# Latent attention in pairs of heads: weights normalised on GpSimd, values stationary in the two column halves of TensorE

## The chip, the cores and the metric

The kernel runs on one core of one Trainium2 chip. A core has TensorE (matrix products; PE in the profile, with PEld for the loading of its stationary operand), VectorE (DVE), ScalarE (ACT), GpSimd (POOL), SyncE (SP, which issues the loads here) and 16 DMA engines. Matrix products are written to PSUM, in banks of 128 partitions by 512 floats. Everything else lies in SBUF. The metric is the device time of one execution in microseconds (us), lower is better.

## The reference

Two decoder layers on 512 positions of width 1024, in float32. Each layer is a feed-forward network, a token mixer and a second feed-forward network, each between RMS norms. The mixer of the first layer is multi-head latent attention, and only that mixer is touched:

```python
def causal_block_attention(q, k, v, scale):      # 512 positions, 16 heads, q and k 96 wide, v 64 wide
    ...
    def one_block(args):                         # 128 queries at a time
        qi, n = args
        s = jnp.einsum('bhqd,bhkd->bhqk', qi, kt).astype(jnp.float32) * scale
        qpos = n * Q_BLOCK + jnp.arange(Q_BLOCK)
        s = jnp.where(kpos[None, :] <= qpos[:, None], s, -jnp.inf)
        p = jax.nn.softmax(s, axis=-1).astype(vt.dtype)
        return jnp.einsum('bhqk,bhkd->bhqd', p, vt)
    ...

def mla(h, w_in, q_norm, w_q_up, kv_norm, w_kv_up, w_o):
    ...
    o = causal_block_attention(q, k, v, (QK_NOPE + QK_ROPE) ** -0.5)
    return o.reshape(B, S, MLA_HEADS * V_HEAD) @ w_o
```

## The kernel before

Activations are kept transposed: a tile has 128 features in its partitions and the 512 positions in its columns. The big products (lines 121 to 123, `mm3`) split each float32 operand into a rounded part and a rest and add three products in the fast type fp32r. The latent attention's own products, its scores, transposes and weighted sums, are plain float32: the compiler makes two passes of each float32 product, and one of a transpose.

The stage begins with `values` (lines 606 to 618), which puts the values of all 16 heads in SBUF as tiles `v`, with 128 positions in the partitions and 64 columns for a head. `keys` (620 to 650) makes the queries and keys of four heads at a time, in five units: one of them, `rope`, has a multiplication on POOL (line 641) for which DVE waits (line 644), and the pairs with keys copy the rotary part on POOL (line 634). `rest` (717 to 736) walks through the heads. For each head it calls `attend` four times, for the query blocks i = 0 to 3. Block i has 128 queries and, since attention is causal, n = 128(i + 1) keys. Between these calls it lets `keys` for the next four heads go on by a unit (after every second call: `KQ`).

`attend` cuts the work on a block into steps that `Pipe(1)` puts one call apart:

- `score` (660 to 669): the product of queries and keys on PE into a bank `mm`, one DVE instruction that scales, masks and finds the row's maximum (666, with a short read of the accumulator), and the exponential on ACT, which also sums the row (669, again with a read of the accumulator). The result is in a tile `sq` (four buffers), with queries in the partitions.
- `turn` (671 to 681): i + 1 transposes on PE into a bank `aux` (676), and a copy to SBUF, on DVE for i < 3 (681) and on ACT for i = 3 (679).
- `weigh` (683 to 705): i + 1 products on PE with a turned 128x128 block of weights as the stationary operand and 64 columns of `v` as the moving one (687). The 128 queries stand in the partitions of the result. After i = 3, DVE takes the reciprocals of the four row sums (696) and multiplies the head's whole output by them (700) into half of a tile `acc`.
- `close` (707 to 713): after every second head, four transposes of `acc` on PE (712) and `put_o` (540 to 546), which splits the result in its rounded part (ACT, 543) and rest (DVE, 544) for the output product.

`rest` then goes on with the output product (`out_unit`), which needs the outputs of all heads. The order of instructions on each engine is set at build time by a scheduler of the framework, which moves instructions past one another as their data allow. Each engine then runs its own queue in that order.

In the second layer the dilated attention has products (line 872) that use 64 of TensorE's 128 rows, a head in each half, and a multiplication on POOL by a broadcast operand (line 985). The change does not touch them, but the prediction reads their prices.

Of the kernel before, what the change touches and what calls it, by code (L numbers as in the profile page):

```python
# [7 lines left out]
F32 = mybir.dt.float32  # L8
F32R = mybir.dt.float32r
AF = mybir.ActivationFunctionType  # L10
ALU = mybir.AluOpType
# [16 lines left out]
KQ = 2  # L28
# [520 lines left out]
class Mla(Mixer):  # L549
# [102 lines left out]
    def attend(self, h, q, k, pipe, at):  # L652
        t, nc = self.t, self.t.nc
        sc = 96.0**-0.5
        if at == 0:
            self.st = t.tmp.tile([P, 8], F32, tag="st", name="st", bufs=3), {}
        st, box = self.st
        nm, z = st[:, 0:4], st[:, 4:8]

        def score(i):  # L660
            n = (i + 1) * P
            c = slice(i, i + 1)
            s = t.bank()[:, :n]
            nc.tensor.matmul(s, q[0:96, i * P : n], k[0:96, :n], start=True, stop=True)  # L664
            p = box[i] = t.t("sq", SB)[:, :n]
            nc.vector.tensor_tensor_reduce(
                p, s, self.mask[:, SEQ - n :], -sc, 3e38, ALU.add, ALU.min, accum_out=nm[:, c]
            )
            nc.scalar.activation(p, p, AF.Exp, bias=nm[:, c], scale=-1.0, accum_out=z[:, c])

        def turn(i):
            n = (i + 1) * P
            x = t.bank("aux")[:, :n]
            for j in range(i + 1):
                r = slice(j * P, (j + 1) * P)
                nc.tensor.transpose(x[:, r], box[i][:, r], t.ident)  # L676
            box[i] = t.t("silu" if i % 2 else "gg")[:, :n]
            if i == 3:
                nc.scalar.activation(box[i], x, AF.Copy)
            else:  # L680
                nc.vector.tensor_copy(box[i], x)

        def weigh(i):
            if i == 0:
                box["o"] = t.bank("aux")
            for j in range(i + 1):
                nc.tensor.matmul(  # L687
                    box["o"][:, i * 64 : i * 64 + 64],
                    box[i][:, j * P : (j + 1) * P],
                    self.v[j, h // 8][:, (h % 8) * 64 : (h % 8) * 64 + 64],  # L690
                    start=j == 0,
                    stop=j == i,
                )
            if i < 3:
                return
            nc.vector.reciprocal(z, z)
            if h % 2 == 0:
                self.os = t.t("acc")
            dst = self.os.rearrange("p (i e c) -> p i e c", i=4, e=2)[:, :, h % 2, :]
            nc.vector.tensor_tensor(  # L700
                dst,
# [438 lines left out]
```

## Time and profile before

| | |
|---|---|
| median of 3 runs | 2410.98 us (2410.79 to 2415.25) |
| span of the profiled execution | 2412.5 us, 0.06% above the median |
| the attention's blocks, first score to last transposes of the output | about 474 to 602 us of the span |
| TensorE busy over the span | 2348.5 us (97%) |
| mean granted TensorE clock | 0.990 |

The page and the trace give no time beside the span, so the span is taken as the profiled execution's own time. Two cautions on reading them. A matmul's recorded duration contains its way through the array, which the next one overlaps: what one costs in a dense stream is the distance between the starts of neighbours. And rows of the time line are merged: `x8` is eight passes in a row that begin at the time given, and the next row's start tells when the stream has moved on.

### The profile page before, as it was taken

How to read it: one execution, taken by the hardware profiler on the slowest of the kernel's cores; microseconds unless marked ns; L12 is line 12 of the kernel's file. 1: busy time of each engine (PE TensorE's matmuls, PEld its weight loads, DVE VectorE, ACT ScalarE, POOL GpSimd, SP SyncE). 2: the span in 40 equal slices, each digit the busy share in tenths (PEclk: the TensorE clock that was granted, in tenths of full speed). 3: DMA queues.
4: the chain of work that ended last, by engine and by line, in shares of the span. 5: the costliest groups of instructions: out<-in, count | busy, mean ns of one | idle time of the engine just before them, and what ended most of it. 6: DMA issues, size and time to landing. Idle time of an engine off the chain costs nothing.

```text
span 2412.5 us, 32825 instructions
## 1 busy us (share of the span) xinstructions
PE 2348.5 (97%) x12430; PEld 1995.6 (83%) x12430; DVE 1235.7 (51%) x2863; ACT 867.2 (36%) x1743; POOL 226.8 (9%) x264
## 2 busy tenths in 40 slices
PE   6999999999999999999999999999999999999998
PEld 5888888778888888888888887888888888888887
DVE  8735536688464454485454364443334456423333
ACT  3422224455432222342222254443334445322221
POOL 0000004210320000230000130000000004100002
PEclk9999999899999999999999999999999998999999
DMA  7645431422245453245454222222222212322221
GB/s 298 220 153 168 158 98 64 151 81 89 70 158 174 151 173 125 68 149 175 148 179 144 89 75 87 70 78 87 87 64 77 88 52 71 105 96 89 104 87 36
DMA packets 104770, 279.46 MB, mean 116 GB/s; under 512 B 28561, under 2 KB 34980, under 8 KB 104612
## 3 DMA queue, kind: packets, MB, share of 16 engines
q1 hardware_dynamic: 104612, 277.36, 35.3%
q8 instruction: 98, 1.61, 0.3%
q14 instruction: 60, 0.49, 0.1%
HBM read 274.95 MB, written 2.37 MB: 115 GB/s over the span
## 4 chain that ended last, share of the span: by engine, by line
PE 89%; DVE 4%; POOL 3%; issue 1%; ACT 1%; DMA 1%; SPq 0%; POOLq 0%; ACTq 0%; DVEq 0%
PE mm L121 26%; PE mm L122 26%; PE mm L123 26%; PE mm L872 2%; PE aux L920 2%; PE mm L664 1%; PE aux L687 1%; PE aux L907 1%; POOL rs L216 1%; DVE x L363 1%; DVE s L360 1%; PE aux L219 1%; PE aux L676 1%; DMA s<-w_mod 1%; POOL sq L250 1%
## 5 line engine op out<-in xcount | busy, mean ns | idle before, releaser
L121 PE MATMUL mm<-s,whi 128*128 128x512 f32 (+1 forms) x3344 | 1214.2, 365 | 8.2 <-ACT whi L104 3.2
L122 PE MATMUL mm<-s,whi 128*128 128x512 f32 (+1 forms) x3344 | 1214.2, 364 | 2.4 <-POOL s L276 1.9
L123 PE MATMUL mm<-s,wlo 128*128 128x512 f32 (+1 forms) x3344 | 1210.1, 363 | 0.0
L104 ACT ACTIVATE whi<-raw 128x1024 fp32r<-128x1024 f32 (+1 forms) x374 | 387.9, 1038 | 1195.1 <-PE mm L122 903.9
L106 DVE TENSOR_TENSOR wlo<-raw,whi 128x512 fp32r<-128x512 f32 (+1 forms) x748 | 489.2, 689 | 538.8 <-ACT whi L104 534.0
L121 PEld LDWEIGHTS mm<-s,whi 128*128 128x128 f32 x3344 | 635.2, 190 | 107.6 <-ACT whi L104 4.0
L122 PEld LDWEIGHTS mm<-s,whi 128*128 128x128 f32 x3344 | 636.4, 190 | 98.7 <-POOL s L276 4.0
L123 PEld LDWEIGHTS mm<-s,wlo 128*128 128x128 f32 x3344 | 635.9, 190 | 94.3 <-DVE wlo L106 0.8
L129 DVE CUSTOM_DVE_ANT_0 raw<-raw,cs 128x1024 f32<-128x1024 f32 x128 | 157.5, 1232 | 147.4 <-DMA raw<-w_mod 146.9
L376 POOL TENSOR_TENSOR acc<-acc,sq 128x256 f32<-128x256 f32 (+1 forms) x60 | 57.5, 959 | 1394.1 <-ACT sq L230 1393.0
L450 DVE TENSOR_TENSOR gg<-silu,mm 128x512 f32<-128x512 f32 (+1 forms) x95 | 60.4, 636 | 174.2 <-PE mm L123 172.5
L476 DVE TENSOR_TENSOR s<-mm,s 128x512 f32<-128x512 f32 (+1 forms) x84 | 47.3, 563 | 144.3 <-PE mm L123 143.8
L887 ACT ACTIVATE sq<-sq,dst 128x128 f32<-128x128 f32 x192 | 79.7, 418 | 8.8 <-DVE dst L880 7.6
L273 ACT ACTIVATE s<-u,mS 128x256 fp32r<-128x256 f32 (+1 forms) x88 | 42.6, 518 | 57.2 <-DVE u L269 57.2
L451 ACT ACTIVATE s<-gg 128x512 fp32r<-128x512 f32 (+1 forms) x97 | 57.4, 592 | 15.3 <-DVE gg L450 13.5
L872 PE MATMUL mm<-s 64*128 64x128 f32 (+1 forms) x384 | 62.7, 321 | 0.0
L230 ACT ACTIVATE sq<-s 128x256 f32<-128x256 f32 (+1 forms) x82 | 35.9, 444 | 59.9 <-DVE s L476 56.9
L453 DVE TENSOR_TENSOR s<-gg,s 128x512 fp32r<-128x512 f32 x79 | 54.2, 686 | 0.3
L880 DVE CUSTOM_DVE_ANT_0 sq<-mm,s 128x128 f32<-128x128 f32 x192 | 51.7, 318 | 4.1 <-PE mm L872 4.1
L448 ACT ACTIVATE silu<-mm 128x512 f32<-128x512 f32 (+1 forms) x95 | 51.3, 540 | 6.4 <-PE mm L123 6.3
L872 PEld LDWEIGHTS mm<-s 64*128 64x128 f32 x384 | 44.1, 186 | 10.8 <-issue 3.4
L363 DVE TENSOR_TENSOR x<-x,s 128x256 f32<-128x256 f32 x90 | 50.0, 586 | 0.0
(149 smaller groups left out, 1542.3 us busy)
## 6 DMA issues: line engine op xcount, KB each, us to landing
raw<-w_gu SPq DMA_DIRECT2D x176, 512.0 KB, 3.3
raw<-w_mod SPq DMA_DIRECT2D x128, 512.0 KB, 3.3
raw<-dil_in SPq DMA_DIRECT2D x72, 512.0 KB, 3.2
raw<-w_down SPq DMA_DIRECT2D x64, 448.0 KB, 3.3
raw<-w_down SPq DMA_DIRECT2D x32, 512.0 KB, 3.6
s<-w_mod SPq DMA_DIRECT2D x32, 256.0 KB, 7.2
raw<-mla_o SPq DMA_DIRECT2D x8, 512.0 KB, 3.7
raw<-dil_o SPq DMA_DIRECT2D x8, 512.0 KB, 3.3
```

What stands on the lines that cost most here:

```text
L104: self.nc.scalar.activation(hi, raw, AF.Copy)
L106: self.nc.vector.tensor_tensor(lo[:, r], raw[:, r], f(hi[:, r]), ALU.subtract)
L121: mm(out, w[0], m[0], start=first, stop=False)
L122: mm(out, w[0], m[1], start=False, stop=False)
L123: mm(out, w[1], m[0], start=False, stop=last)
L129: nc.vector.tensor_tensor_reduce(raw, raw, self.cs, 1.0, 0.0, ALU.mult, ALU.add, accum_out=t[:, 0:1])
L363: eng.tensor_tensor(self.x[:, k, lo:hi], self.x[:, k, lo:hi], yk, ALU.add)
L376: nc.gpsimd.tensor_tensor(acc, acc, self.sq(yk, n), ALU.add)
L450: nc.vector.tensor_tensor(v, s, banks[1], ALU.mult)
L451: nc.scalar.activation(ghi, v, AF.Copy)
L872: nc.tensor.matmul(s[:, at : at + n], q[rows, i * P : (i + 1) * P], k[rows, k0 : k0 + n], start=True, stop=True)
L887: nc.scalar.activation(y[:, c], y[:, c], AF.Exp, bias=st[:, g, i, e : e + 1], scale=-1.0, accum_out=st[:, g, i, 2 + e : 3 + e],)
```

## The change

Heads are worked on in pairs, and `attend` is called for a pair c and a block i.

- `score` makes both heads' scores, maxima and exponentials. Then DVE takes the reciprocals of both row sums, and POOL multiplies each `sq` tile by its reciprocal, broadcast along the row. The weights are thus normalised before they are turned.
- `turn` turns both heads' weights, into tiles `silu` (first head) and `gg` (second).
- `weigh` has 64 columns of `v` as the stationary operand and the turned weights, 128 queries, as the moving one. The first head's result goes to partitions 0 to 63 of the bank and the second's to 64 to 127, so that each head uses one half of TensorE's columns. The result has features in its partitions and 128 queries in its columns, and after i = 3 `put_o` reads it as it is: the step `close`, its transposes, and the multiplication of line 700 are gone.
- `rest` calls `keys` on after each of the eight calls for a group of four heads (before: after every second of sixteen).

```diff
-    def attend(self, h, q, k, pipe, at):
+    def attend(self, c, q, k, pipe, at):
 ...
         def score(i):
             n = (i + 1) * P
-            c = slice(i, i + 1)
-            s = t.bank()[:, :n]
-            nc.tensor.matmul(s, q[0:96, i * P : n], k[0:96, :n], start=True, stop=True)
-            p = box[i] = t.t("sq", SB)[:, :n]
 ...
-            nc.scalar.activation(p, p, AF.Exp, bias=nm[:, c], scale=-1.0, accum_out=z[:, c])
+            nm, z, r = [st[:, i, 2 * x : 2 * x + 2] for x in range(3)]
+            box[i] = []
+            for e in range(2):
+                s = t.bank()[:, :n]
+                nc.tensor.matmul(s, q[e][0:96, i * P : n], k[e][0:96, :n], start=True, stop=True)
+                p = t.t("sq", SB)[:, :n]
 ...
+                nc.scalar.activation(
+                    p, p, AF.Exp, bias=nm[:, e : e + 1], scale=-1.0, accum_out=z[:, e : e + 1]
+                )
+                box[i].append(p)
+            nc.vector.reciprocal(r, z)
+            for e in range(2):
+                p = box[i][e]
+                nc.gpsimd.tensor_tensor(p, p, r[:, e : e + 1].to_broadcast([P, n]), ALU.mult)
 ...
         def weigh(i):
             if i == 0:
                 box["o"] = t.bank("aux")
             for j in range(i + 1):
-                nc.tensor.matmul(
-                    box["o"][:, i * 64 : i * 64 + 64],
-                    box[i][:, j * P : (j + 1) * P],
-                    self.v[j, h // 8][:, (h % 8) * 64 : (h % 8) * 64 + 64],
-                    start=j == 0,
-                    stop=j == i,
-                )
-            if i < 3:
-                return
-            nc.vector.reciprocal(z, z)
 ...
-        def close(i):
-            if i == 3 and h % 2:
-                x = t.bank("aux")
-                for j in range(4):
-                    r = slice(j * P, (j + 1) * P)
-                    nc.tensor.transpose(x[:, r], self.os[:, r], t.ident)
-                self.put_o(x)
+                for e in range(2):
+                    h = 2 * c + e
+                    nc.tensor.matmul(
+                        box["o"][64 * e : 64 * e + 64, i * P : (i + 1) * P],
+                        self.v[j, h // 8][:, (h % 8) * 64 : (h % 8) * 64 + 64],
+                        box[i][e][:, j * P : (j + 1) * P],
+                        start=i == j == 0,
+                        stop=i == j == 3,
+                        skip_group_check=True,
+                    )
+            if i == 3:
+                self.put_o(box["o"])
```

A constant at the top is dropped, so the lines of the changed kernel stand one lower than before up to `attend`: its line 120 is 121 before, 640 is 641. In `attend` the changed kernel's lines are 664 (score), 666 (maximum), 669 (exponential), 673 (reciprocal), 676 (multiplication on POOL), 684 (transposes), 687 and 689 (copies), 698 (weighted sums) and 707 (`put_o`).

On TensorE, this is a piece of the last quarter of the heads, where no key units are left to fill in (a number behind a name is a buffer's; buffers named `s` hold queries, keys, values and the mask). Before, with two query blocks of a head and the end of a pair:

```order
L687 MATMUL aux_4880<-s_3775,gg_4891 128x64
L687 MATMUL aux_4880<-s_3803,gg_4891 128x64
L676 MATMUL aux_4916<-ident_76,sq_4898 128x128
L687 MATMUL aux_4880<-s_3747,silu_4906 128x64
L687 MATMUL aux_4880<-s_3775,silu_4906 128x64
L687 MATMUL aux_4880<-s_3803,silu_4906 128x64
L687 MATMUL aux_4880<-s_3832,silu_4906 128x64
L676 MATMUL aux_4931<-ident_76,sq_4913 128x128 x2
L664 MATMUL mm_4961<-s_4600,s_4596 128x128
L687 MATMUL aux_4936<-s_3747,gg_4918 128x64
L664 MATMUL mm_4976<-s_4600,s_4596 128x256
L712 MATMUL aux_4938<-ident_76,acc_4868 128x128 x4
```

Now, from the scores of block i = 3 of a pair on:

```order
L664 MATMUL mm_4859<-s_4266,s_4262 128x512
L664 MATMUL mm_4864<-s_4267,s_4263 128x512
L684 MATMUL aux_4846<-ident_76,sq_4802 128x128 x2
L684 MATMUL aux_4851<-ident_76,sq_4807 128x128 x2
L698 MATMUL aux_4856<-silu_4815,s_3747 64x128
L698 MATMUL aux_4856<-gg_4819,s_3747 64x128
L664 MATMUL mm_4889<-s_4595,s_4591 128x128
L664 MATMUL mm_4894<-s_4596,s_4592 128x128
L698 MATMUL aux_4856<-silu_4849,s_3747 64x128
L684 MATMUL aux_4872<-ident_76,sq_4835 128x128 x3
L684 MATMUL aux_4878<-ident_76,sq_4840 128x128 x3
L698 MATMUL aux_4856<-gg_4854,s_3747 64x128
```

Each step is now done for two heads in a row, and the weighted sums alternate between the heads, in runs between products that use the full array. There are 41 such runs of line 698 in the program, with 160 products (320 passes) in all: ten runs of one product, eight of 2, four of 3, five of 4, three each of 5 and 6, seven of 8, and one of 13. After the rows shown come two more products of line 698, two scores of 256 columns, six products of line 698 and one score of 384, and then the eight transposes of `sq_4861` and `sq_4866`, the weights that the scores in the first two rows give.

On VectorE at the same place, now (an `ISA` row of line 666 with `sq` is the maximum, the one after it the read of the accumulator):

```order
L673 RECIPROCAL st_4754<-st_4754 128x2
L689 COPY silu_4849<-aux_4846 128x256
L689 COPY gg_4854<-aux_4851 128x256
L666 ISA sq_4861,st_4754<-mm_4859,s_3218 128x512
L666 ISA st_4754 128x1
L666 ISA sq_4866,st_4754<-mm_4864,s_3218 128x512
L666 ISA st_4754 128x1
L689 COPY silu_4876<-aux_4872 128x384
L689 COPY gg_4882<-aux_4878 128x384
L673 RECIPROCAL st_4754<-st_4754 128x2
```

and before (lines 129, 132 and 179 make scale factors for later norms, which is filler here):

```order
L666 ISA sq_4779,st_4761<-mm_4777,s_3218 128x256
L666 ISA st_4761 128x1
L681 COPY gg_4784<-aux_4782 128x128
L696 RECIPROCAL st_4674<-st_4674 128x4
L179 SCALAR_TENSOR_TENSOR mG_87<-mt_5323,small_74 128x1
L132 TENSOR_TENSOR mt_5329<-mt_5329,small_74 128x1
L129 ISA raw_5333,mt_5335<-raw_5333,cs_71 128x1024
L129 ISA mt_5335 128x1
L700 TENSOR_TENSOR acc_4704<-aux_4735,st_4674 128x4x64
L179 SCALAR_TENSOR_TENSOR mG_87<-mt_5329,small_74 128x1
L132 TENSOR_TENSOR mt_5335<-mt_5335,small_74 128x1
```

Now each block has a reciprocal (`st_4754`, first for i = 2 and then for i = 3). It stands behind copies of the block before it, and POOL's multiplications wait for it; the multiplication of line 700 is gone.

On GpSimd, before, at the keys of the last group of heads:

```order
L634 TENSOR_SCALAR s_4269<-s_3325 32x512
L641 TENSOR_TENSOR u_4335<-u_4335,s_3217 128x512
L634 TENSOR_SCALAR s_4270<-s_3325 32x512
L634 TENSOR_SCALAR s_4271<-s_3325 32x512
L634 TENSOR_SCALAR s_4599<-s_3325 32x512
L634 TENSOR_SCALAR s_4600<-s_3325 32x512
L641 TENSOR_TENSOR u_4666<-u_4666,s_3217 128x512
L634 TENSOR_SCALAR s_4601<-s_3325 32x512
```

Now:

```order
L676 TENSOR_TENSOR sq_4619<-sq_4619,st_4557 128x256
L676 TENSOR_TENSOR sq_4624<-sq_4624,st_4557 128x256
L640 TENSOR_TENSOR u_4661<-u_4661,s_3217 128x512
L633 TENSOR_SCALAR s_4597<-s_3325 32x512
L676 TENSOR_TENSOR sq_4671<-sq_4671,st_4557 128x384
L676 TENSOR_TENSOR sq_4676<-sq_4676,st_4557 128x384
L633 TENSOR_SCALAR s_4598<-s_3325 32x512
L676 TENSOR_TENSOR sq_4716<-sq_4716,st_4557 128x512
L676 TENSOR_TENSOR sq_4721<-sq_4721,st_4557 128x512
```

The 64 multiplications of the weights stand among the instructions for the keys. SyncE's queue is the same before and now, and on the other engines the order differs only within this stage.

More of the change, by code (lines that the diff above doesn't have):

```diff
@@ L27 @@
 TAIL = 5
-KQ = 2
 UB = 4
@@ L726, in rest @@
             q, k = self.qk[g]
-            for j in range(4):
+            for j in range(2):
                 for i in range(4):
-                    self.attend(4 * g + j, q[j], k[j], pipe, i)
-                    if (4 * j + i) % KQ == KQ - 1:
-                        next(ahead, None)
+                    self.attend(2 * g + j, q[2 * j : 2 * j + 2], k[2 * j : 2 * j + 2], pipe, i)
+                    next(ahead, None)
             for _ in ahead:
```

40 lines of the change are left out of this document (16 added, 24 removed).

## Prediction

> **What bounds the kernel now.** I read the page first, then the stage of the change: its windows, its part of the chain, and its groups. The page says whose time counts:
>
> ```profile
> span 2412.5 us, 32825 instructions
> PE 2348.5 (97%) x12430; PEld 1995.6 (83%) x12430; DVE 1235.7 (51%) x2863; ACT 867.2 (36%) x1743; POOL 226.8 (9%) x264
> ```
>
> PE is busy for 97% of the span. The windows of the attention's blocks (first, last, sum; PE, PEld, DVE, ACT, POOL busy):
>
> ```profile
> 474.00:500.00 26.00, 23.80 (x124) 18.08 (x123) 23.09 (x56) 12.41 (x29) 6.96 (x7) 0.93 0.18 61
> 575.00:602.00 27.00, 27.00 (x194) 23.01 (x193) 21.98 (x75) 14.51 (x40) 0.00 (x0) 1.00 0.26 85
> sum 128.00, PE 124.59 PEld 100.57 DVE 111.23 ACT 66.90 POOL 15.48; mean PE 24.92 PEld 20.11 DVE 22.25 ACT 13.38 POOL 3.10
> ```
>
> The stage is 128 us long. PE is its bound, but DVE, at 111 us, is close behind, while POOL has 112 us free. The start has idle PE time, the last window none. The groups of the stage count what the change touches (busy, mean ns of one, idle before):
>
> ```profile
> L676 PE MATMUL aux<-ident,sq 128*128 128x128 f32 x160 | 27.5, 275 | 1.2 <-ACT sq L669 1.2
> L687 PE MATMUL aux<-s,silu 128*128 128x64 f32 x192 | 26.0, 268 | 0.0
> L687 PE MATMUL aux<-s,gg 128*128 128x64 f32 x128 | 18.1, 262 | 0.0
> L666 DVE CUSTOM_DVE_ANT_0 sq<-mm,s 128x512 f32<-128x512 f32 x16 | 10.9, 684 | 1.6 <-PE mm L664 1.0 <-PE aux L676 0.5
> L700 DVE TENSOR_TENSOR acc<-aux,st 128x256 f32<-128x256 f32 x16 | 6.8, 423 | 5.6 <-PE aux L687 5.3
> L696 DVE RECIPROCAL st<-st 128x4 f32<-128x4 f32 x16 | 2.8, 172 | 0.0
> L669 ACT ACTIVATE sq<-sq,st 128x512 f32<-128x512 f32 x16 | 11.5, 717 | 6.2 <-DVE st L666 6.2
> L669 ACT ACTIVATION_READ_ACCUMULATOR sq<-sq,st 128x1 f32 x64 | 12.0, 188 | 0.0
> ```
>
> The busy times of PE contain overlaps, so prices of a pass come from the time line, by the distance from start to start:
>
> ```profile
> 586.70 1.02 PE L664 MATMUL mm<-s 96*128 96x512 f32 x2
> 587.56 0.71 PE L676 MATMUL aux<-ident,sq 128*128 128x128 f32 x5
> 588.10 0.82 PE L664 MATMUL mm<-s 96*128 96x128 f32 x4
> 588.76 0.78 PE L687 MATMUL aux<-s,gg 128*128 128x64 f32 x6
> 589.38 1.06 PE L687 MATMUL aux<-s,silu 128*128 128x64 f32 x8
> 590.27 0.39 PE L676 MATMUL aux<-ident,sq 128*128 128x128 f32 x2
> 590.50 0.34 PE L687 MATMUL aux<-s,gg 128*128 128x64 f32 x2
> 590.67 0.86 PE L664 MATMUL mm<-s 96*128 96x384 f32 x2
> 591.37 0.60 PE L712 MATMUL aux<-ident,acc 128*128 128x128 f32 x4
> 591.81 0.38 PE L676 MATMUL aux<-ident,sq 128*128 128x128 f32 x2
> ```
>
> Five transposes take 0.54 us (588.10 - 587.56), 0.108 each. The weighted sums, with 64 columns to stream, take hardly less: 16 passes in 0.62 + 0.89 + 0.17 = 1.68 us, 0.105 each.
>
> **PE: what goes.** 320 passes of line 687 at 0.105 are 33.6 us. The 32 transposes of line 712 at 0.11 (four in 0.44) are 3.5. Together 37.1 us, all on the bound.
>
> **PE: what comes.** Again 320 passes, but with 128 columns to stream: 0.108 each, as for the transposes. Nothing is won unless the two column halves run at the same time. No row of this trace has column halves. The nearest rows are those of the dilated scores, which use row halves, a head in each:
>
> ```profile
> 1478.42 0.48 PE L872 MATMUL mm<-s 64*128 64x128 f32 x2
> 1478.83 0.33 PE L907 MATMUL aux<-ident,sq 128*128 128x128 f32 x1
> 1479.09 0.71 PE L872 MATMUL mm<-s 64*128 64x128 f32 x4
> 1479.73 0.44 PE L907 MATMUL aux<-ident,sq 128*128 128x128 f32 x2
> 1549.57 0.94 PE L872 MATMUL mm<-s 64*128 64x128 f32 x10
> 1550.44 0.44 PE L907 MATMUL aux<-ident,sq 128*128 128x128 f32 x2
> ```
>
> They show two things. Four passes of one head take 0.64 us up to the next product, ten of both heads 0.87: halves do run at the same time, since six more passes in line would have cost 0.65. And going from the full array to a half and back costs time: from 1478.42 to 1479.09 three passes take 0.67 us, 0.34 more than three of 0.11. A product with 16 stationary columns, the only one with few, bounds that from the other side:
>
> ```profile
> 1453.12 0.39 PE L122 MATMUL mm<-s,whi 128*128 128x512 f32 x1
> 1453.35 0.39 PE L123 MATMUL mm<-s,wlo 128*128 128x512 f32 x1
> 1453.67 2.10 PE L760 MATMUL aux<-s,u 33*16 33x384 f32 x6
> 1455.70 0.50 PE L121 MATMUL mm<-s,whi 128*128 128x512 f32 x1
> 1456.04 0.39 PE L122 MATMUL mm<-s,whi 128*128 128x512 f32 x1
> ```
>
> An fp32r pass takes 0.23 (1453.12 to 1453.35). The one before the change of tile takes 0.32, the one after it 0.34, and the six between take 2.03, 0.10 over six of 0.32 (three quarters of the 0.43 that line 664 takes for 512 columns, two in 0.86 from 586.70). That is 0.09 + 0.11 + 0.10. So a round trip is 0.30 to 0.34; I take 0.31, as 64 columns are loaded and not 128.
>
> The order has 41 runs of line 698. A run of n products has 2n passes, n in each half; with one pass of skew it takes n + 1 slots. That is 160 + 41 = 201 slots of 0.108, or 21.7 us, and 41 x 0.31 = 12.7 for the switches: 34.4 us. PE's work thus changes by 34.4 - 37.1 = -2.7 us. Nearly all that the halves win, the switches take back. Ends of this term: with no switch price and no skew 160 x 0.108 = 17.3 (-19.8 us); with halves that run one after the other 34.6 + 12.7 = 47.3 (+10.2).
>
> On loading, TensorE: Matmul & The Clock Gate (Part 3, The mechanism), of the Trainium skill, says that a weight load overlaps running matmuls only when their row groups differ. Column halves share their row groups, so by that rule loads would stand between the passes; with about 0.05 for 64 columns (half of 0.10, an estimate) the new sums would cost some 16 us more. The trace speaks against it: the five transposes above share all rows, each has a load, and they still come 0.108 apart. So I don't take it.
>
> **The path to the transposes gets longer.** Before, a block's weights were ready after ACT. Now a reciprocal on DVE waits for both heads' exponentials, and two multiplications on POOL follow. Their price is in three rows:
>
> ```profile
> L376 POOL TENSOR_TENSOR acc<-acc,sq 128x256 f32<-128x256 f32 x48 | 38.9, 810 | 50.5 <-ACT sq L230 49.5
> L376 POOL TENSOR_TENSOR acc<-acc,sq 128x512 f32<-128x512 f32 x12 | 18.6, 1553 | 1343.6 <-ACT sq L230 1343.5
> L985 POOL TENSOR_TENSOR s<-s,w 128x512 f32<-128x512 f32 x14 | 14.6, 1044 | 214.7 <-DMA w<-w 214.5 <-POOL s L985 0.2
> ```
>
> Line 985 also multiplies by a broadcast operand, so it is nearest: 1.04 us for 512 columns, and by the slope of line 376 about 0.4, 0.6 and 0.83 for 128, 256 and 384. A pair has 2 x 2.87 = 5.7 us of them, 46 us in all beside the 15.5 that POOL has: it is no bound. But 0.17 + 2 x 1.04 = 2.25 us stand in the way of the transposes of i = 3, and 1.0 to 1.8 of the others.
>
> Does the order cover that? I walk through the piece shown, from the end of the second 512 score. PE's next work up to `sq_4861`'s transposes: ten transposes 1.1, four runs of 2, 1, 3 and 6 products 16 x 0.108 + 4 x 0.31 = 3.0, scores of 128, 256 and 384 columns for 0.44 + 0.87 + 0.65: 6.1 us. The other side: 0.68 + 0.08 on DVE and 0.72 + 0.19 on ACT end at 1.7, but the reciprocal stands behind the copies of the block i = 2, whose transposes run at 2.0 to 2.7; so it ends at about 3.8, POOL at 4.9 and 5.9. PE wants the first head at 6.1 and the second at 6.5: in time, the second by 0.6 us. With the 2.25 us less of the kernel before there is far more room. So I expect short waits, at one or two of the four blocks of a pair, where DVE or POOL is late: 0.3 to 0.5 per pair, 3 us for eight. At the end of the stage nothing stands between the last transposes and the last sums: 1.5 us. The ends of this term are 0 and, were half the added 1.0 to 2.25 (mean 1.6) of 32 steps bare, 26 us.
>
> **DVE and POOL hinder each other.** The additions of the rope, 32 x 512, read two tiles of SBUF, as two other groups of the stage do:
>
> ```profile
> L129 DVE CUSTOM_DVE_ANT_0 raw<-raw,cs 128x1024 f32<-128x1024 f32 x14 | 17.0, 1217 | 0.0
> L106 DVE TENSOR_TENSOR wlo<-raw,whi 128x512 fp32r<-128x512 f32 x12 | 7.9, 680 | 0.0
> L644 DVE TENSOR_TENSOR s<-u x16: 682/1000/1007, 471.6 to 556.5; 32x512 f32<-32x512 f32 x16
> ```
>
> Line 644 takes 0.68 at the least, with little POOL work beside it, and 1.00 in the median, beside the copies of line 634. The three groups are some 40 instructions. With POOL busy half the time, about 20 would take 0.3 more, 6 us on an engine that loses 9.6 (lines 696, 700) and gets 32 x 0.17 = 5.4 for the reciprocals. DVE thus stays at about 113 of 128 us; I count 1 us for PE. Also line 641's product queues behind two or four multiplications on POOL, and DVE's line 644 waits for it in order, with the maxima behind it: 0 to 1.2 us at three places, of which I take 1 in all.
>
> The scores, maxima, exponentials, copies and `put_o` stay as many as they were. Keys still come as five units in the first calls of a group, SP's queue doesn't change, and no load is later. These cost nothing; PE's fp32r work beside them hides the rest as before.
>
> **Sum.** -2.7 + 3 + 1.5 + 1 + 1 = +3.8 us, about 2416 on the span of 2412.5. The runs' median is 1.5 us below that span, so the forecast is 2414.5. A change under 0.2%, 4.8 us, is what a measurement can't tell from none.
>
> **Rivals.**
>
> - The halves run one after the other: +10.2 from PE, and with PE later the waits shrink to perhaps 4. That is +14, 2425. For it: no row has column halves, and both read all 128 rows, where row halves read 64 each. Against it: the ten passes in 0.87.
> - POOL's multiplications stand in the way at each block, slower than in line 985 because DVE hinders them: a third of 32 x 1.6 us, 17, less 2.7: 2425 to 2428. This decides as soon as a step's bare wait is over 0.25 us (8 in 32 steps). For it: DVE at 87% and reciprocals behind copies. Against it: the walk.
> - On the other side, the switches are hidden by loads and skew, half of their 12.7 or more, and the order covers the chain: -2.7 - 6.4 - 4.4 (the skew of 41 slots) + 3 = -10, 2400. For it: a weighted sum streams from both halves at once, and the first window's idle PE time could take some of the new work. Against it: the price at 1478.42 and at 1453.67, in two kinds of tiles. The Trainium skill's TensorEngine Tiling (When to Use Tiling) goes further: with 64 moving columns, swap and use column tiling for up to twice the speed. By it the 33.6 us halve and the stage loses 20 us, 2391 if nothing waits; no run here shows that yet.
>
> **How the numbers follow.** The forecast case (halves at once, switches at the price of the rows, waits of 0 to 13 us) has 0.5: within 0.2% 0.30, slower 0.17, faster 0.03. Serial halves 0.15 and POOL in the way 0.13, both slower. The switches hidden 0.22: 0.17 faster, 0.05 within. That makes 0.20 faster, 0.35 the same, 0.45 slower: the forecast lies inside the band, with more beyond its upper edge than below its lower. For the range I leave out a tenth below 2402 and a tenth above 2428.
>
> **What would show it.** Right: starts of line 698 that come in pairs a few ns apart, a run of eight in about 1.0 to 1.3 us, some 0.2 us at each change to line 684 or 664, POOL at 60 us in the stage, transposes that wait for POOL for a few us in all. Wrong: runs of eight in 1.8 us (serial halves), or PE waiting for POOL or the reciprocals for over 10 us, or switches without a gap.

## The result and the profile after

The change makes the kernel slower by 0.6%: median 2426.06 us of 4 runs (2419.71 to 2431.34) against 2411.59, ratio 1.0057 with a 95% interval of 1.0039 to 1.0076. The forecast was 2414.5, its range 2402 to 2428. The time lies at the upper edge of the range, and it is the time that a rival had named, not the forecast. A second timing of the same kernel (e5) came to 2428.5, just above the range.

The page of the changed kernel (span 2412.5, PE 2348.5, POOL 226.8 before):

```profile
span 2423.8 us, 32856 instructions
PE 2350.5 (97%) x12398; PEld 1978.0 (82%) x12398; DVE 1238.2 (51%) x2863; ACT 867.0 (36%) x1743; POOL 283.8 (12%) x328
```

The attention's blocks by line (shortest, median and longest in ns, then first and last start), before:

```profile
L664 PE MATMUL mm<-s x128: 272/483/842, 474.5 to 593.4; 96*128 96x128 f32 x32, 96*128 96x256 f32 x32, 96*128 96x384 f32 x32, 96*128 96x512 f32 x32
...
L712 PE MATMUL aux<-ident,acc x32: 270/273/282, 501.2 to 602.1; 128*128 128x128 f32 x32
```

Now, and windows of the stage:

```profile
L664 PE MATMUL mm<-s x128: 272/483/697, 474.3 to 604.3; 96*128 96x128 f32 x32, 96*128 96x256 f32 x32, 96*128 96x384 f32 x32, 96*128 96x512 f32 x32
L698 PE MATMUL aux<-gg,s x160: 272/273/324, 485.7 to 612.1; 128*64 128x128 f32 x160
```

```profile
474.00:500.00 26.00, 19.67 (x93) 13.15 (x91) 22.12 (x57) 11.49 (x28) 13.12 (x13) 0.93 0.17 57
...
sum 138.00, PE 124.65 PEld 81.83 DVE 113.16 ACT 66.49 POOL 71.94; mean PE 41.55 PEld 27.28 DVE 37.72 ACT 22.16 POOL 23.98
```

From the first score to the end of the last sum the stage took 127.9 us before; now it takes 138.1 (474.3 to 612.4). That is 10.2 of the 11.3 us by which the span grew. PE's busy time in it is the same (124.6), so PE stands still for about 13 us where it stood for 3. In the first window alone it is busy for 19.7 us where it was 23.8. What it waits for, in the list of waits of the stage (us in all, times, longest):

```profile
POOL sq L676 <- DVE st L673: 56.2, 22, 6.8
...
PEld aux L684 <- POOL sq L676: 19.8, 33, 4.5
...
PE aux L684 <- POOL sq L676: 9.6, 14, 4.3
```

PE and its loads now wait for POOL's multiplications: the loads for 19.8 us, the products for 9.6. The two counts overlap (the stop of 4.3 us shown below is in both), so they can't be added: TensorE itself stands idle for POOL for 9.6 of its 13 us, and the loads' 19.8 are the fuller measure of the wait, which is used from here on. (The expectations of the experiments add the two.) Before, the loads waited for the exponentials, 4.6 us by the same count:

```profile
PEld aux L676 <- ACT sq L669: 4.6, 8, 1.7
...
PE aux L676 <- ACT sq L669: 1.2, 3, 0.9
```

The groups of the stage (busy, mean ns of one, idle before):

```profile
L684 PE MATMUL aux<-ident,sq 128*128 128x128 f32 x160 | 27.8, 287 | 10.1 <-POOL sq L676 9.6
...
L676 POOL TENSOR_TENSOR sq<-sq,st 128x512 f32<-128x512 f32 x16 | 23.0, 1458 | 7.6 <-DVE st L673 5.3 <-PE mm L664 1.5 <-PE mm L122 0.7
...
L128 DVE CUSTOM_DVE_ANT_0 raw<-raw,cs 128x1024 f32<-128x1024 f32 x14 | 17.1, 1224 | 0.0
...
L676 POOL TENSOR_TENSOR sq<-sq,st 128x384 f32<-128x384 f32 x16 | 13.4, 856 | 21.3 <-DVE st L673 21.3
...
L676 POOL TENSOR_TENSOR sq<-sq,st 128x128 f32<-128x128 f32 x16 | 12.3, 791 | 9.4 <-DVE st L673 9.1 <-DVE mt L131 0.2
...
L105 DVE TENSOR_TENSOR wlo<-raw,whi 128x512 fp32r<-128x512 f32 x12 | 9.7, 825 | 0.0
...
L676 POOL TENSOR_TENSOR sq<-sq,st 128x256 f32<-128x256 f32 x16 | 9.5, 615 | 23.8 <-DVE st L673 20.5 <-PE aux L698 2.3 <-PE mm L122 0.9
```

The multiplications of 256 and 384 columns cost what the prediction priced (0.6 and 0.83); those of 512 (1.46 for 1.04) and, above all, of 128 columns (0.79 for 0.4) do not. The line's own row and the largest stop say why:

```profile
L676 POOL TENSOR_TENSOR sq<-sq,st x64: 395/827/4994, 482.4 to 608.3; 128x128 f32<-128x128 f32 x16, 128x256 f32<-128x256 f32 x16, 128x384 f32<-128x384 f32 x16, 128x512 f32<-128x512 f32 x16
```

```profile
494.93 6.71 POOL L676 TENSOR_TENSOR sq<-sq,st 128x512 f32<-128x512 f32 x4 [0.74 <-PE mm L122]
...
496.33 1.21 DVE L128 CUSTOM_DVE_ANT_0 raw<-raw,cs 128x1024 f32<-128x1024 f32 x1
...
497.55 1.27 DVE L105 TENSOR_TENSOR wlo<-raw,whi 128x512 fp32r<-128x512 f32 x2
...
498.81 1.21 DVE L128 CUSTOM_DVE_ANT_0 raw<-raw,cs 128x1024 f32<-128x1024 f32 x1
...
500.98 1.09 PE L684 MATMUL aux<-ident,sq 128*128 128x128 f32 x4 [4.30 <-POOL sq L676]
```

The second multiplication of this row took 4.99 us. It lies beside four DVE instructions that each read two tiles of SBUF, 1.21 + 1.27 + 1.21 = 3.69 us; with its free 1.04 that makes 4.73. On DVE, line 128 keeps its time (1.224 us, before 1.217), and line 105 pays a little (0.825 us, before 0.680). So POOL stands while such an instruction runs, and here it got no turn between one and the next. Of the 64 multiplications ten took over 0.1 us more than the free prices above, 13.4 us in all, and each of the ten lies beside line 128 or line 105.

The sums themselves did what they were made for. A run of eight products, 16 passes:

```profile
540.52 0.38 PE L684 MATMUL aux<-ident,sq 128*128 128x128 f32 x2
540.84 0.32 PE L698 MATMUL aux<-silu,s 128*64 128x128 f32 x1
540.84 0.32 PE L698 MATMUL aux<-gg,s 128*64 128x128 f32 x1
541.00 0.27 PE L698 MATMUL aux<-silu,s 128*64 128x128 f32 x1
541.00 0.27 PE L698 MATMUL aux<-gg,s 128*64 128x128 f32 x1
...
541.65 0.27 PE L698 MATMUL aux<-silu,s 128*64 128x128 f32 x1
541.66 0.27 PE L698 MATMUL aux<-gg,s 128*64 128x128 f32 x1
541.86 3.27 PE L664 MATMUL mm<-s 96*128 96x384 f32 x8
```

The two halves start together, and the run takes 1.02 us (540.84 to 541.86); 16 passes in line would take 1.74.

### The profile page after: what moved, and what is told of

It reads as the page before. It is cut to its first block, busy times and chain, and to the rows that moved or that the text cites. A ratio compares the mean times of both kernels' runs of the same rounds, so it can differ in the third digit from the quotient of the medians.

```text
span 2423.8 us, 32856 instructions
## 1 busy us (share of the span) xinstructions
PE 2350.5 (97%) x12398; PEld 1978.0 (82%) x12398; DVE 1238.2 (51%) x2863; ACT 867.0 (36%) x1743; POOL 283.8 (12%) x328
## 4 chain that ended last, share of the span: by engine, by line
PE 88%; DVE 5%; POOL 4%; issue 2%; ACT 1%; DMA 1%; SPq 0%; POOLq 0%; DVEq 0%; ACTq 0%
PE mm L120 26%; PE mm L121 26%; PE mm L122 26%; PE mm L865 2%; PE aux L913 2%; POOL sq L676 1%; PE aux L900 1%; POOL rs L215 1%; PE aux L218 1%; DVE s L359 1%; DVE x L362 1%; POOL sq L249 1%; PE aux L684 1%; PE aux L698 1%; PE mm L664 1%
## 5 line engine op out<-in xcount | busy, mean ns | idle before, releaser
L676 POOL TENSOR_TENSOR sq<-sq,st 128x128 f32<-128x128 f32 (+3 forms) x64 | 58.1, 930 | 62.1 <-DVE st L673 56.2
```

Of the source, the lines that this page charges most:

```text
L676: nc.gpsimd.tensor_tensor(p, p, r[:, e : e + 1].to_broadcast([P, n]), ALU.mult)
```

## The experiments

Theory 1: what costs is latency. A block's weights now pass from the exponential through a reciprocal that waits for both heads and through POOL, and one step of distance between scores and transposes does not cover that. Theory 2: what costs is POOL's time, since DVE's instructions with two operands in SBUF stop it. A third question is what the column halves are worth by themselves.

All kernels are timed against the kernel before on the same chip. A kernel's runs spread over some 10 us with the granted clock (before: 2409.1 us at 0.994, 2418.8 at 0.987), so the length of the stage in the profiled execution is read first and the ratio second. The stage runs from the first score's start to the end of the last sums (of the last output transposes, where those remain). In all of these executions TensorE has run the same 2192 products before it starts. Its length has two weaknesses. The granted clock within the stage was 0.98 to 1.00 in most executions, but 0.97 in e11, 0.96 in e9, 0.95 in e3 and 0.92 in e8, so that these four may read too long, e8 by up to 7% (the ratio of the clocks, an estimate). And the scheduler doesn't put quite the same number of the big products into the stage: each of the lines 121 to 123 (now 120 to 122) stands there 44 times before, 42 times in the changed kernel and in e7, and 40 times in e1.

| kernel | stage, us | median of runs, us | ratio to before, 95% |
|---|---|---|---|
| before | 127.9 | 2411.59 to 2414.26 | 1 |
| the changed kernel | 138.1 | 2426.06 | 1.0057 (1.0039 to 1.0076) |
| e5, the same again | 136.3 | 2428.54 | 1.0058 (1.0042 to 1.0074) |
| e1, no normalisation | 120.1 | 2412.18 | 0.9992 (0.9979 to 1.0005) |
| e2, normalisation on ACT | 131.9 | 2418.34 | 1.0020 (1.0009 to 1.0030) |
| e3, before with POOL's normalisation | 150.9 | 2436.91 | 1.0100 (1.0087 to 1.0113) |
| e4, DVE's filler with one operand | 130.8 | 2419.63 | 1.0018 (1.0005 to 1.0030) |
| e6, head after head | 141.9 | 2431.73 | 1.0074 (1.0061 to 1.0087) |
| e7, distance 2 | 118.2 | 2404.34 | 0.9963 (0.9951 to 0.9975) |
| e8, diagonal matrix | 135.7 | 2419.71 | 1.0032 (1.0017 to 1.0047) |
| e9, before with distance 2 | 131.6 | 2416.54 | 1.0014 (1.0001 to 1.0027) |
| e10, buffers only | 137.8 | 2425.71 | 1.0051 (1.0032 to 1.0070) |
| e11, distance 3 | 119.5 | 2410.92 | 0.9991 (0.9979 to 1.0003) |
| e12, e7 without normalisation | 113.5 | 2404.42 | 0.9961 (0.9950 to 0.9973) |

**e1: without the normalisation** (the division is left out).

```diff
-            nc.vector.reciprocal(r, z)
-            for e in range(2):
-                p = box[i][e]
-                nc.gpsimd.tensor_tensor(p, p, r[:, e : e + 1].to_broadcast([P, n]), ALU.mult)
```

> The changed kernel without the reciprocals and without POOL's multiplications (the softmax's division is left out). Both theories of the loss, POOL starved by VectorE's two-operand instructions (port) and a chain that is too long in itself (chain), put all of it on the path of the normalisation: the halves run at once and save TensorE about 6 us, so 2404 to 2408 us, below the kernel before. If the tile switches or the scheduling in pairs were to blame instead, it stays at 2415 or more.

```profile
L664 PE MATMUL mm<-s x128: 272/483/697, 475.4 to 590.1; 96*128 96x128 f32 x32, 96*128 96x256 f32 x32, 96*128 96x384 f32 x32, 96*128 96x512 f32 x32
...
L694 PE MATMUL aux<-gg,s x160: 272/273/324, 486.3 to 595.2; 128*64 128x128 f32 x160
```

The stage falls to 120.1 us, 7.8 under before. Read as it stands, column halves, the dropped transposes and the work in pairs save 8 us, and the normalisation costs 16 to 18 (to 136.3 and 138.1). But e1 has 12 big products fewer in its stage than before and 6 fewer than the changed kernel; at 0.23 us each (1453.12 to 1453.35 in the prediction's rows) 2.8 and 1.4 us have only moved behind the stage. That leaves some 5 us saved and 15 to 17 of cost. The total gains less than the stage: 0.08%, with no change in its interval. What follows the stage took 1820.7 us in the profiled execution for 1810.1 before, with these products more and at a lower clock (0.985 over the execution, before 0.990), and the runs of e1 were granted 0.989 in the median, those of before 0.990. At an equal 0.992 e1 took 2405 to 2408 us and before 2411.7 to 2413.9, some 6 apart, which agrees with the 5.

**e2: the multiplication on ACT.**

```diff
-                nc.gpsimd.tensor_tensor(p, p, r[:, e : e + 1].to_broadcast([P, n]), ALU.mult)
+                nc.scalar.activation(p, p, AF.Copy, scale=r[:, e : e + 1])
```

> The changed kernel with the 64 multiplications on ScalarE (a copy with a scale per row) instead of GpSimd. The chain stays as long, 0.4 to 0.7 us a multiplication and on an engine that is busy for 70 of 138 us, but ScalarE doesn't contend with VectorE. Port: 2407 to 2414 us. Chain: 2418 to 2426, as now.

131.9 us, and a total at the lower edge of the chain's range; by the ratio, set against the 2411.59 from which the expectation was written, it is 2416.4, between the two. The transposes hardly wait for the multiplications any more, but PE waits elsewhere:

```profile
PEld mm L120 <- DVE st L666: 5.8, 4, 2.7
...
PEld aux L684 <- ACT sq L676: 2.2, 11, 0.3
```

4 to 6 us come back without POOL; 12 of the 16 to 18 do not. How much of these 12 is the longer chain, e2 can't say: ACT is now busy for 94.6 us of the stage, where it was 66.5, and PE's loads wait more for the maxima of line 666 than for the multiplications.

**e3: the normalisation alone, in the kernel before.**

```diff
             nc.scalar.activation(p, p, AF.Exp, bias=nm[:, c], scale=-1.0, accum_out=z[:, c])
+            nc.vector.reciprocal(z[:, c], z[:, c])
+            nc.gpsimd.tensor_tensor(p, p, z[:, c].to_broadcast([P, n]), ALU.mult)
...
-            nc.vector.reciprocal(z, z)
...
-            nc.vector.tensor_tensor(
-                dst,
-                box["o"][:, :256].rearrange("p (i c) -> p i c", i=4),
-                z.unsqueeze(2).to_broadcast([P, 4, 64]),
-                ALU.mult,
-            )
+            nc.vector.tensor_copy(dst, box["o"][:, :256].rearrange("p (i c) -> p i c", i=4))
```

> The kernel before with one part of the change alone: a reciprocal per block and the multiplication of the weights on POOL, head by head; the multiplication of the output becomes a copy; full-width sums and the transposes of the output stay. Port: POOL is starved here too, 2419 to 2426 us. Chain: a step adds 0.17 and one multiplication of 0.4 to 1.04 us, 2413 to 2418.

Worse than both theories said: the stage grows by 23.0 us. The normalisation alone, with no column halves and no pairs, is the whole loss and more. Its waits are those of the changed kernel:

```profile
PEld aux L678 <- POOL sq L671: 24.6, 30, 1.7
```

**e4: DVE's filler with one operand.** The product with c in line 128 is left out; only the sum along the row remains.

```diff
-        nc.vector.tensor_tensor_reduce(
-            raw, raw, self.cs, 1.0, 0.0, ALU.mult, ALU.add, accum_out=t[:, 0:1]
-        )
+        nc.vector.tensor_reduce(t[:, 0:1], raw, mybir.AxisListType.X, ALU.add)
```

> The changed kernel with the 1024-wide product-and-sum of the modulation (14 of them lie in the attention's stage) replaced by a plain sum of one operand of about the same length, at the same places in VectorE's queue; the product with the condition is left out. Port: POOL's multiplications return to 0.40 to 1.04 us, but for those beside line 105 and 643, and the time falls to 2410 to 2418 us. Chain: no change, 2420 to 2428.

```profile
L674 POOL TENSOR_TENSOR sq<-sq,st x64: 398/826/1652, 476.7 to 595.4; 128x128 f32<-128x128 f32 x16, 128x256 f32<-128x256 f32 x16, 128x384 f32<-128x384 f32 x16, 128x512 f32<-128x512 f32 x16
```

```profile
PEld aux L682 <- POOL sq L674: 14.0, 31, 1.0
...
PE aux L682 <- POOL sq L674: 4.4, 13, 0.8
```

The instruction takes as long as before on DVE (1.20 us) and stands as often in the stage (14 times), but POOL's longest multiplication falls from 4.99 to 1.65 us, the loads' waits from 19.8 to 14.0, and the stage by 5.5 to 7.3 us. (A short read of the accumulator, 0.08 us, goes with the product.) What POOL's multiplications take over their free prices falls from 13.4 to 3.5 us, all of it beside line 105, which still has two operands. It is the second operand that stops POOL. The total, 2419.6, lies between the two ranges. Some 9 to 11 us of the normalisation's cost are still there (130.8 against e1's 120.1, with and without 6 big products).

**e5: the changed kernel again.**

> The changed kernel as it is, timed in the same job as the three below, so that each can be set against it at equal granted clock. All theories: 2420 to 2430 us, first score to last sum about 138 us. What it tells: whether the 4.5 us stop of TensorE early in the stage and the clock of 0.79 after it come back (if so they belong to the order of the instructions and not to that one run).

As expected; the stop of 4.3 us is there again, at the same place in the order, and with it a fall of the clock just after (0.60 in the 4 us from 498 on; 0.88 and 0.69 in the first execution):

```profile
498.00:502.00 4.00, 3.31 (x10) 2.80 (x11) 0.00 (x0) 0.60 (x1) 1.97 (x4) 0.60 0.72 260
```

**e6: one head's products after the other's.**

```diff
-            for j in range(i + 1):
-                for e in range(2):
+            for e in range(2):
+                for j in range(i + 1):
```

> The two inner loops of the sums are swapped: all key tiles of head 0, then all of head 1, so that neighbouring products go to the same half of TensorE's columns. Theory 1 (two products in different halves run side by side, the second of a pair starts 7 ns after the first): nearly all pairs are lost, 320 passes x 0.109 = 34.9 us take the place of the 26.7 us start to start, and at most some of it falls into waits that are there anyway: stage 142 to 148 us, total 2428 to 2438. Theory 2 (the short distance of the starts is how the trace models them, and the halves share the array's time): the order of the loops is indifferent: stage 136 to 140 us, total as the changed kernel, within 3 us of it.

```profile
536.11 0.54 PE L698 MATMUL aux<-silu,s 128*64 128x128 f32 x3
536.38 0.32 PE L698 MATMUL aux<-gg,s 128*64 128x128 f32 x1
536.49 0.27 PE L698 MATMUL aux<-silu,s 128*64 128x128 f32 x1
536.54 0.27 PE L698 MATMUL aux<-gg,s 128*64 128x128 f32 x1
...
536.71 0.27 PE L698 MATMUL aux<-silu,s 128*64 128x128 f32 x1
536.76 0.49 PE L698 MATMUL aux<-gg,s 128*64 128x128 f32 x3
```

The order matters: the stage is 4 to 6 us longer, just under theory 1's range, and the total is at the low end of theory 1. Passes to one half come 0.109 apart (536.49 to 536.71 is two of them), and only neighbours in different halves overlap. From start to start line 698 takes 32.6 us in the stage, in the changed kernel 27.1; a full loss of the overlap would have made it 34.9 and the ends of the runs. The halves still overlap in part: the kernel writes three products of the first head and then three of the second, and the second head's first pass starts (536.38) while three of the first head's six are still to come.

**e7: distance 2.** Four blocks can be open, and the transposes come two steps after the scores.

```diff
-                p = t.t("sq", SB)[:, :n]
+                p = t.t("u" if e else "sq", 4)[:, :n]
...
-        pipe = Pipe(1)
+        pipe = Pipe(2)
```

> Transposes of a block come two steps after its scores and not one, and the weights of the second head lie in the pool u, so that four blocks can be open at once where two could. All of the arithmetic stays. Theory 1 (of the 18 us that the normalisation adds to the stage, what is not POOL's slowing beside DVE's two-operand instructions, about 11 us, is the longer chain exponential, reciprocal, multiplication, which one step of distance doesn't cover; the slowed multiplications are latency too and would be covered with it): stage 122 to 130 us, waits of the transposes for POOL under 8 us, total 2411 to 2419. Theory 2 (POOL and DVE are short of throughput, so that distance only moves the wait): stage 134 to 140 us, total within 4 us of the changed kernel.

```profile
L676 POOL TENSOR_TENSOR sq<-sq,st 128x384 f32<-128x384 f32 x8 | 8.8, 1099 | 17.8 <-DVE st L673 13.8 <-DVE mt L131 3.5 <-PE aux L684 0.6
...
L676 POOL TENSOR_TENSOR sq<-sq,st 128x256 f32<-128x256 f32 x8 | 7.2, 894 | 14.9 <-DVE st L673 5.9 <-DVE mt L131 3.3 <-PE mm L664 3.0
```

```profile
PEld aux L684 <- POOL u L676: 1.3, 3, 0.6
...
PEld aux L684 <- POOL sq L676: 0.7, 2, 0.5
```

POOL's multiplications are still stopped (1.10 and 0.89 us for 0.83 and 0.61), but hardly anybody waits: the loads 2.0 us in place of 19.8. The stage takes 118.2 us, under the 122 to 130 of theory 1. With the whole computation this version is faster than both kernels: 0.9963 (0.9951 to 0.9975).

**e8: a diagonal matrix in place of the unit matrix.**

```diff
-                nc.gpsimd.tensor_tensor(p, p, r[:, e : e + 1].to_broadcast([P, n]), ALU.mult)
+                x = d[:, e * P : e * P + P]
+                nc.gpsimd.tensor_tensor(x, t.ident, r[:, e : e + 1].to_broadcast([P, P]), ALU.mult)
+                box[i].append(x)
...
-                    nc.tensor.transpose(x[:, r], box[i][e][:, r], t.ident)
+                    nc.tensor.matmul(x[:, r], box[i][e][:, r], box[i][2 + e], start=True, stop=True)
```

(`d` is a tile of the rounded type; the maximum writes to a tile of its own, and the exponential rounds the weights.)

> The normalisation is put into the transposes: POOL multiplies a unit matrix of 128 columns by the reciprocals (64 x 0.40 = 26 us at its free price in place of 47 us), and a product of the weights with this diagonal matrix, in the rounded fp32 type with one pass, takes the place of the transpose; the weights are rounded to that type. Theory 1 (what costs is the chain's length and POOL's work): the multiplication of 512 columns (1.04 us and more) leaves the chain, the passes cost what the transposes cost or less: stage 122 to 130 us, total 2411 to 2419. Theory 2 (what costs is that POOL is stopped beside DVE's two-operand instructions, however short its own instruction is: those of 128 columns took 0.79 us on average for 0.40): 64 multiplications stay exposed to it: stage 130 to 136 us, total 2418 to 2425. If a pass of 128 columns in the rounded type is cheaper than a transpose (0.109 us), 5 to 8 us less by either.

```profile
L678 POOL TENSOR_TENSOR acc<-ident,st 128x128 fp32r<-128x128 f32 x64 | 34.1, 553 | 79.8 <-DVE st L674 69.4 <-DVE mA L173 5.0 <-PE mm L664 3.4
...
L687 PEld LDWEIGHTS aux<-acc,sq 128*128 128x128 f32 x160 | 24.5, 210 | 14.5 <-POOL acc L678 11.8 <-issue 0.5
```

135.7 us, the upper end of theory 2, at a low clock in this stage; the total, 2419.71 at a granted 0.990 in the median, is in theory 2's range too. The loads' waits for POOL fall from 19.8 to 11.8 us, since the multiplications are short. Neighbouring products with the diagonal start 0.115 us apart in the median, the transposes of the changed kernel 0.110, so the hope of 5 to 8 us from cheaper passes was wrong. Why the stage gives back less than the waits isn't settled: from start to start the products take 27.4 us, the transposes of e5 31.9, but the weighted sums behind them 30.4 for 27.1, and the clock was lower.

**e9: the kernel before with distance 2** (`Pipe(2)` and nothing else).

> The kernel before, its arithmetic and order untouched but for the distance: a block's transposes come two steps after its scores and not one (its pool sq holds four blocks of one head). Theory 1 (the distance pays because it covers the chain exponential, reciprocal, multiplication of the changed kernel): before had no such chain, its transposes and their loads waited 6.4 us for the exponentials, so at most that comes back: stage 121 to 128 us (before: 127.9), total 0 to 6 us under before. Theory 2 (the distance fills gaps of any kind in this stage, and the changed order and column halves have no part in it): the stage falls here by as much as from the changed kernel to its version of distance 2, to 108 to 112 us, total 12 us or more under before.

```profile
PEld aux L687 <- DVE gg L681: 7.0, 6, 2.4
```

Neither: the stage grows by 3.7 us, of which the lower clock (0.96 for 0.99) may be most, and the total by 0.14%. The waits for the exponentials go, but others come, for the copies of the turned weights. Distance by itself brings nothing here; theory 2 is refuted.

**e10: the buffers of e7 at distance 1.**

> The changed kernel with the weights of the second head in the pool u, so that four blocks can be open, but with the distance of one step left as it is. Theory 1 (the distance is what covers the chain): stage 133 to 139 us (changed kernel: 136.3 and 138.1), waits of the transposes and their loads for POOL 22 us or more, total within 4 us of the changed kernel. Rival (with four buffers for two heads a third block's scores wait for a buffer, and that is what was short): stage 118 to 126 us, total 2404 to 2414.

137.8 us and 1.0051: buffers were not what was short; the distance is.

**e11: distance 3.**

```diff
-        pipe = Pipe(2)
+        pipe = Pipe(3)
```

> As the version of distance 2 with buffers for four blocks, but distance 3. Theory 1 (at 2 the transposes' waits for POOL are down to 2.7 us, TensorE bounds the stage): nothing is left for more distance, stage 116 to 121 us (at 2: 118.2), total within 3 us of 2404. Rival (what idle time TensorE has left at 2 is the chain too): stage 112 to 116 us, total 2398 to 2401.

119.5 us in the stage, as theory 1 says. The total, 2410.92, is 4 us over its margin. Its runs were granted 0.988 in the median and those of e7 0.992; at 0.989, where both have runs, they took 2409.3 and 2409.7 against 2408.3. In the profiled executions the first score came at 476.4 us and in e7 at 470.4, after the same products and at a granted 0.98 for 1.00, so more than the whole difference of the two (2407.8 and 2403.7) lies ahead of the stage. So distance 3 is no gain; whether it is a loss stays open.

**e12: e7 without the normalisation** (the division is left out, as in e1).

> The version of distance 2 without reciprocals and multiplications: the division by the sums is left out. At distance 1 leaving it out took 16 to 18 us off the stage (136.3 and 138.1 to 120.1). Theory 1 (that was latency, and at distance 2 it is covered): stage 115 to 119 us, 0 to 3 us under the 118.2 with normalisation. Rival (part of it was work that stands in TensorE's way at any distance, DVE and POOL being short of time): stage 107 to 113 us.

113.5 us, between the two ranges: 4.7 under e7 in the length of the stage, at a slightly higher clock in it (1.00 for 0.99). The totals are equal (0.9961 and 0.9963). At distance 2 the normalisation costs at most 5 us of the stage, and nothing that the totals show; at distance 1 it was 15 to 18.

## Why the prediction was right, and where it was not

The time lies in the range and on the forecast's side, but not by the forecast's mechanism. Two terms were far off in opposite directions, and the larger one pushed the time to the edge of the range; that it stayed inside is in part luck. The prediction's own sign of being wrong, over 10 us of waiting for POOL, was there at the loads (19.8 us), and nearly so in TensorE's idle time (9.6).

- **PE, what goes (37.1 us).** Start to start, line 687 took 32.2 us in the stage and line 712 3.5: 35.7. The prices held.
- **PE, what comes (34.4 us).** The slot price (0.108, measured 0.109) and the halves at once were right. The mis-sized part is what a run costs at its ends. I counted one pass of skew, 0.11, and 0.31 for the switch. The run shown has no skew, since both heads' passes start together, and its ends cost 0.10 (540.52 to 540.84 for two transposes), 0.05 (0.16 between the first two passes) and 0.10 (0.21 at the end): 0.25. With that, 160 x 0.109 + 41 x 0.25 = 27.7 us (an estimate, since it takes the ends of one run for all 41), and the term is 27.7 - 35.7 = -8.0 for -2.7. e1 gives -7.8, or some -5 without the products that moved. The Trainium skill's TensorEngine Tiling (Array Packing), in Theoretical Speedup and When to Use Tiling, gives up to twice the speed for such a swap. The run of eight has 1.74 to 1.02, 1.7 times; over the stage, with short runs, the sums go from 32.2 to 27.7, 1.2 times.
- **The longer path (3 us, 26 at the most).** This is the step that failed: 19.8 us of waits of the transposes' loads for POOL, and 15 to 18 us of the stage by e1. Two things were wrong in it. The walk took POOL at its free price, where it is stopped by DVE (5.5 to 7.3 us by e4). And it took the queues as if each engine were at the place the walk begins with; one step of distance leaves 9 to 11 us of the chain bare even when POOL runs nearly freely (e4), and two steps cover it (e7), which buffers alone don't (e10). Which of the links of that chain costs how much of it was not taken apart.
- **DVE and POOL hinder each other (1 us).** The mechanism was seen in the right rows and put on the wrong engine. DVE is as busy as forecast (113.2 us): its line 128 keeps its time, and the 0.145 us that each of the 12 instructions of line 105 pays are 1.7 us. POOL pays more: 71.9 us busy in the stage for the forecast 61.5.
- **The rope's queue (1 us)** cost nothing: DVE waited 2.4 us for line 640, before 3.1 for the same instruction. **The stage's end (1.5 us)**: 0.7 us of waiting before the last transposes but eight; then products of the output filled in.
- **Sum.** With the measured sizes: -8 + 18 = +10, which is the stage (by construction, since both are read against e1). The rest of the 14.5 us between the medians is clock: at a granted 0.990 the changed kernel took 2425.6 and 2426.5 us, and before 2413.1 to 2416.8, some 11 us apart. Whether the change itself lowers the clock, by stops like the one of 4.3 us, is not settled: e4 has no such stop, and was granted 0.986 to 0.994 as well.
- **The rivals.** Serial halves are refuted by the run of eight and by e6. Hidden switches are half right (the -8), but the whole is no gain. POOL in the way at each block, slower because DVE hinders it, is what happened, with its time (2425 to 2428) and its condition: the bare wait per step is 9.6 / 32 = 0.3 us on TensorE itself and 19.8 / 32 = 0.6 at its loads, over the 0.25 that it asked for. It had 0.13. The walk that spoke against it covered one place of the order at undisturbed prices, and that was not enough to weigh so much.

The Trainium skill's SBUF — State Buffer (Who interferes with whom) says that a DVE instruction with two SBUF inputs and a GpSimd instruction that reads SBUF exclude each other for a whole instruction, and that a reduction with one input does not. The stop of 4.99 us for 3.69 + 1.04, line 105's 0.825 us for 0.680 and e4's 1.65 agree. The prediction did not use it.

## What to carry to other kernels

Work that is moved to an idle engine is free only if the order leaves room for its latency: here the same multiplications cost 15 to 18 us of the stage at one step of distance and at most 5, with nothing in the total, at two. Before giving POOL work that someone waits for, count the DVE instructions with two SBUF operands that run beside it, above all filler that comes in a row, because POOL waits out the whole row. When a change joins a gain on the bound (here 5 to 8 us) with a longer chain, price the two apart, and look for the distance that covers the chain.

## What had not been expected of the hardware

- A POOL multiplication of 128 columns, 0.40 us when free, took 3.74 us, beside three of DVE's line 128 with only short instructions between them; POOL did not get in between. The row holds it and the next one, which was free:

```profile
570.76 4.10 POOL L676 TENSOR_TENSOR sq<-sq,st 128x128 f32<-128x128 f32 x2 [0.23 <-DVE mt L131]
```

- TensorE seems not to keep the queue's order between the two column halves: in e6 a pass of the second head started (536.38) before three passes of the first (536.49 to 536.71), which stand ahead of it in the order that the kernel writes. The order of that run's queue itself is not on record.
- The load of a 128x128 block takes 0.14 us for a transpose and 0.19 for a product, in float32 (0.192 for line 687 before) and in the rounded type fp32r (0.192 in the median in e8) alike.
- After a stop of 4.3 us the granted clock fell to 0.69 and 0.60 in a window of 4 us, once TensorE worked again:

```profile
498.00:502.00 4.00, 1.02 (x5) 1.03 (x6) 2.03 (x5) 0.00 (x0) 3.91 (x4) 0.88 0.78 227
502.00:506.00 4.00, 4.00 (x14) 3.13 (x13) 0.12 (x1) 1.49 (x2) 0.34 (x1) 0.69 0.42 166
```
